# A hybrid attention layer on one core: weight preparations ordered behind earlier evacuations, with small edits at the start and the end

## The chip, the cores and the metric

The kernel runs on one core of one Trainium2 chip. The metric is the device time of one launch in microseconds, as the median of the runs that are shown. The engines are TensorE (PE in the rows, with its weight loads as PEld), VectorE (DVE), ScalarE (ACT), GpSimd (POOL) and SyncE (SP), which issues most of the DMA transfers. Each engine works through its own list of instructions in the order in which they stand in the program; across engines they wait for each other through semaphores.

## What is computed

One encoder layer runs on 512 tokens (256 of a prompt, 256 of a sample, each with 1024 channels). Everything is float32.

```python
h = _rmsnorm(x, attn_norm_gain)
proj = h @ w_in            # q,k,v; decay/beta; gates; latents; memory query; 3 merge gates
qkv = _centred_conv_silu(qkv, conv_w)
o_fwd = _gdn_chunked(q, k, v, g[:, :, 0], beta[:, :, 0])
o_bwd = _gdn_chunked(q[:, ::-1], k[:, ::-1], v[:, ::-1], g[:, ::-1, 1], beta[:, ::-1, 1])[:, ::-1]
o_gdn = _rmsnorm(o_fwd + o_bwd, gdn_norm_gain).reshape(b, s, W_GDN) * jax.nn.silu(z_gdn)
o_mla = _blocked_attention(q_full, k_full, v_mla, (D_NOPE + D_ROPE) ** -0.5).reshape(b, s, W_MLA) * jax.nn.silu(z_mla)
o_mem = jnp.einsum("bhqk,bkhd->bqhd", p, vm).reshape(b, s, W_MEM) * jax.nn.silu(z_mem)
merged = gates[:, :, 0] * (o_gdn @ w_br_gdn) + gates[:, :, 1] * (o_mla @ w_br_mla) + gates[:, :, 2] * (o_mem @ w_br_mem)
return x + merged @ w_out   # then a final RMSNorm
```

Branch A is a bidirectional gated delta rule in chunks of 64 tokens with 8 heads, branch B a latent attention (MLA) with 8 heads, branch C an attention of 4 heads into 256 memory tokens for each half.

## The kernel before

**Products in three passes.** To keep float32 accuracy on fp32r operands, every operand of a product is held as a rounded high part and a low part, which is the remainder. A product is high x high, then low of the data x high of the weight, then high of the data x low of the weight: for a contraction of 1024 and 128 output channels that is 3 x 8 matmuls of 128x512 into one PSUM bank. In names, `wh_`/`wl_` are the parts of a weight and `hh`/`hl` those of the normalised input.

**A weight's way.** `weight()` (line 224) brings a weight of up to 128x1024 with one SP DMA into one of two raw buffers (`wr_...`), has ACT round it (`wh_...`, line 241) and has DVE subtract to get the low part (`wl_...`, line 244). Both are issued with a raised priority. `gemm()` (line 264) then issues the matmuls (line 276). The finished bank is evacuated, depending on the kind of product: `split()` makes a high part on ACT (line 252) and a low part on DVE (line 254) for the values `v`, keys `kn` and queries `qn` of MLA; the convolution copies it into `cz_...` on ACT (line 767) and goes on with taps on DVE and ACT (lines 769 to 778); gates get a tanh on ACT (lines 1223 and 1251).

**Stages and what sets the order.** `front()` does the memory values first (`mem_v()`, lines 379 to 430: memory tokens times a weight, with ten matmuls on a zero tile ahead of them), then the norms, latents and the two attentions, with convolution inputs and gates put in between. Here the tile scheduler places the instructions of every engine by its own simulation and by priorities. `middle()` is the delta rule with the remaining projections; its TensorE order is written out by `weave`, from lists of work in which a generator yields when it may go on, while the other engines' orders still come from the scheduler. `back()` has the branch products and `output()`, which multiplies by `w_out`, adds the residual and does the final norm, the last quarter of the tokens in two halves of 256 channels (lines 1383 to 1401). `issue_after(i)` fixes that an instruction stands behind `i` in the program on the same engine; it adds no semaphore.

**Places that the steps below touch.** The rounding and low part in `weight()` (lines 241 and 244); the evacuations named above; `attend` (lines 356 to 367), which multiplies attention weights by values with 12 matmuls of 128x256, of which 4 read the low part `pl_a`; `gdn_out` (line 1182), where a yield of 12 sets how much other TensorE work lies ahead of the matmul `so` (line 1185) that waits for the sum `rr` (line 1181); in `mem_v()` the memsets (lines 383 and 387), the ten `zp` matmuls (line 390) and the load of the parameters `prm` (line 405), which the scaling of the memory tokens reads (lines 419 and 420).

Of the kernel before, what the change touches and what calls it, by code (L numbers as in the profile page):

```python
# [181 lines left out]
class Layer:  # L182
    def __init__(self, tc, A):
        self.tc, self.nc, self.A, self.hold = tc, tc.nc, A, None


# [37 lines left out]
    def weight(self, src, n, name, pool=None, into=None):  # L224

        nc = self.nc
        raw = self.p0.tile([P, 1024], F32, tag="wr", bufs=2, name="wr_" + name)
# [4 lines left out]

        def place(t, own):
            if into is not None:
                return into[t == "wl_"]
            kw = {} if pool else {"tag": own, "bufs": 2}
            return (pool or self.p0).tile([P, 1024], F32R, name=t + name, **kw)

        hi = place("wh_", "wh")
        with self.tc.high_priority(offset=60):  # L240
            self.wround = nc.scalar.activation(hi[:, :n], raw[:, :n], AF.Copy).ins  # L241
            lo = place("wl_", "wl")
            with nullcontext() if self.hold is None else self.tc.issue_after(self.hold):
                self.wsplit = nc.vector.tensor_tensor(lo[:, :n], raw[:, :n], hi[:, :n].bitcast(F32),  # L244
                                                      op=ALU.subtract).ins
            self.hold = None
        return hi, lo

    def split(self, src, hi, lo, scale=1.0):

        nc = self.nc
        a = nc.scalar.activation(hi, src, AF.Copy, scale=scale)
        if isinstance(scale, float) and scale == 1.0:
            self.lsplit = nc.vector.tensor_tensor(lo, src, hi.bitcast(F32), op=ALU.subtract).ins
# [65 lines left out]
    def attend(self, h, s, score, scale, vs, op, name):  # L320
# [40 lines left out]
        self.plast = self.lsplit  # L361
        n = 0
        for kb in range(2):
            q = slice(kb * 256, (kb + 1) * 256)
            for a, b in ((vs[kb][0], hi), (vs[kb][0], lo), (vs[kb][1], hi)):
                nc.tensor.matmul(pairs(op), a, turns(b[:, q]), start=n == 0, stop=n == 5)
                n += 1

# [10 lines left out]
    def mem_v(self):  # L379
        nc, A = self.nc, self.A  # L380
        ms = []
        warm = self.p0.tile([P, 1], F32, name="warm")
        nc.vector.memset(warm, 0.0)
        nc.scalar.activation(warm, warm, AF.Square)

        zero = self.s2("zero", F32R)
        nc.vector.memset(zero.bitcast(F32), 0.0)
        zp = self.ps_kk("zp")
        for i in range(10):
            nc.tensor.matmul(zp, zero[:, 0:P], zero, start=i == 0, stop=i == 9)  # L390

# [312 lines left out]
    def mla_v(self, g):  # L704
# [4 lines left out]
        for tb in range(4):  # L709
# [52 lines left out]
    def conv(self, ps, f, dst, name):  # L762
# [3 lines left out]
        with self.tc.high_priority(offset=60):  # L766
            nc.scalar.activation(z, ps.rearrange("p (s t) -> p s t", s=2), AF.Copy)
        y = dst
# [377 lines left out]
    def gdn_out(self, hh):  # L1146
# [32 lines left out]
        with self.behind():  # L1179
            nc.vector.transpose(out=st, in_=sq)  # L1180
            nc.vector.tensor_reduce(red, st.rearrange("p (j i) -> p j i", i=32), axis=AX.X, op=ALU.add)
        yield 0.0, 13 if hh == 7 else 12
        ssp = self.ps_ms(par, f"so{hh}")
# [36 lines left out]
    def silu2(self, dst, ps):  # L1220

        with self.tc.high_priority(offset=60):
            self.nc.scalar.activation(dst, ps, AF.Tanh, scale=0.5)
            self.nc.vector.scalar_tensor_tensor(dst, dst, 1.0, ps, ALU.add, ALU.mult)

# [19 lines left out]
    def gate(self, j, d):  # L1245
# [4 lines left out]
        with self.tc.high_priority(offset=60):  # L1250
            self.nc.scalar.activation(th, ps, AF.Tanh, scale=0.5)
        return th
# [69 lines left out]
    def output(self):  # L1322
# [399 lines left out]
```

## Time and profile before

| what | value |
|---|---|
| runs | 798.55, 798.67 and 798.84 us, median 798.67 us |
| profiled execution | 798.48 us, of which the span from first to last instruction is 796.7 us |
| granted TensorE clock, mean | 0.999 of full speed |
| PE busy | 786.6 us, 99% of the span, 4774 matmul records |
| PEld busy (beside PE) | 692.9 us, 87% |
| DVE busy | 579.2 us, 73% |
| ACT busy | 447.4 us, 56% |
| POOL busy | 166.9 us, 21% |
| DMA | 118.18 MB, mean 148 GB/s |

A row of the timeline gives start, duration, engine, line, operation, output and inputs, shapes and count (in us); behind it in brackets the idle time of that engine just before and what ended it. Matmuls overlap in the rows: one of 128x512 is shown with 0.38 us and the next starts 0.216 us after it. A row of the waits gives who waited for whom: total, times, longest.

### The profile page before, as it was taken

Reading aid. Unit: us, or ns where it says so; the run is one execution under the profiler, and the core shown is the slowest. Engines: PE = TensorE matmul, PEld = TensorE weight load, DVE = VectorE, ACT = ScalarE, POOL = GpSimd, SP = SyncE. Lnnn points to the kernel's source line nnn. Section 1 sums busy time; section 2 is a strip of 40 time slices with the busy share of each in tenths; the row PEclk is TensorE's granted clock in tenths of the full one; section 3 lists DMA queues with packets and bytes.
Section 4 is the critical chain, followed back from the end, with each engine's and each line's share of the span. In section 5 each row is a group of like instructions: output and inputs, shape, how many; then the busy total and the mean of one; then the engine's idle time right before and its main releaser. Section 6 shows DMA issues by size and latency. Waiting matters only on the chain.

```text
span 796.7 us, 13067 instructions
## 1 busy us (share of the span) xinstructions
PE 786.6 (99%) x4774; PEld 692.9 (87%) x4774; DVE 579.2 (73%) x974; ACT 447.4 (56%) x894; POOL 166.9 (21%) x135
## 2 busy tenths in 40 slices
PE   9999999999999999999999999999999999999996
PEld 7888898889898899988888888888888888888886
DVE  7886358787699999669599989498565655465543
ACT  6755465556565565646757556667766463322332
POOL 0200111000010002154221226540512003333312
PEclk9999999999999999999999999999999999999999
DMA  9523222732417635444444435555653557464532
GB/s 325 177 78 102 93 77 81 229 124 70 116 61 211 192 96 141 142 133 154 129 155 133 146 120 160 172 151 175 192 172 119 172 181 256 160 197 153 178 107 105
DMA packets 68911, 118.18 MB, mean 148 GB/s; under 512 B 23664, under 2 KB 31344, under 8 KB 68848
## 3 DMA queue, kind: packets, MB, share of 16 engines
q1 hardware_dynamic: 67552, 115.03, 45.9%
q10 hardware_dynamic: 1296, 2.33, 0.8%
q8 instruction: 37, 0.61, 0.3%
q14 instruction: 26, 0.21, 0.1%
HBM read 98.24 MB, written 19.09 MB: 147 GB/s over the span
## 4 chain that ended last, share of the span: by engine, by line
PE 91%; DVE 4%; DMA 1%; ACT 1%; issue 1%; POOL 0%; SPq 0%; POOLq 0%; ACTq 0%; DVEq 0%
PE gm_qkv L276 14%; PE gm_g L276 14%; PE gm_z L276 7%; PE gm_za L276 5%; PE gm_bm L276 5%; PE y L1345 5%; PE vm L427 3%; PE gm_be L276 3%; PE gm_qm L276 3%; PE gm_km L276 3%; PE gm_bg L276 3%; PE o L1163 2%; PE gm_bg L1312 2%; PE s_a L330 2%; PE kk L1012 2%; PE gm_qn L276 2%
## 5 line engine op out<-in xcount | busy, mean ns | idle before, releaser
L776 DVE SCALAR_TENSOR_TENSOR kq<-cz,prm,kq 128x510 f32<-128x510 f32 (+1 forms) x64 | 52.0, 813 | 2.2 <-ACT kq L769 1.3
L276 PE MATMUL gm_qkv<-hl,wh_qkv 128*128 128x512 f32 x192 | 49.0, 385 | 0.0
L276 PE MATMUL gm_g<-hh,wl_g 128*128 128x512 f32 x192 | 48.8, 384 | 0.0
L276 PE MATMUL gm_g<-hh,wh_g 128*128 128x512 f32 x192 | 48.0, 385 | 0.0
L276 PE MATMUL gm_g<-hl,wh_g 128*128 128x512 f32 x192 | 47.2, 382 | 0.0
L276 PE MATMUL gm_qkv<-hh,wl_qkv 128*128 128x512 f32 x192 | 47.0, 382 | 0.0
L276 PE MATMUL gm_qkv<-hh,wh_qkv 128*128 128x512 f32 x192 | 46.8, 381 | 0.0
L1287 POOL TENSOR_TENSOR mg<-mg,lg 128x512 f32<-128x512 f32 x16 | 29.5, 1849 | 73.2 <-DVE lg L1286 31.8
L244 DVE TENSOR_TENSOR wl_g<-wr_g,wh_g 128x1024 fp32r<-128x1024 f32 x24 | 31.2, 1300 | 17.1 <-PE gm_g L276 9.3
L244 DVE TENSOR_TENSOR wl_qkv<-wr_qkv,wh_qkv 128x1024 fp32r<-128x1024 f32 x24 | 31.0, 1290 | 13.6 <-ACT wh_qkv L241 7.7
L1022 DVE SCALAR_TENSOR_TENSOR ne<-e,cc,kk 128x512 f32<-128x512 f32 (+1 forms) x64 | 35.7, 608 | 6.2 <-ACT ed L843 2.7
L276 PEld LDWEIGHTS gm_qkv<-hh,wh_qkv 128*128 128x128 f32 x192 | 35.8, 189 | 5.1 <-ACT wh_qkv L241 0.3
L276 PEld LDWEIGHTS gm_g<-hl,wh_g 128*128 128x128 f32 x192 | 35.9, 189 | 4.7
L276 PEld LDWEIGHTS gm_qkv<-hh,wl_qkv 128*128 128x128 f32 x192 | 35.8, 189 | 4.8
L276 PEld LDWEIGHTS gm_g<-hh,wh_g 128*128 128x128 f32 x192 | 35.4, 189 | 4.8
L276 PEld LDWEIGHTS gm_qkv<-hl,wh_qkv 128*128 128x128 f32 x192 | 35.4, 189 | 4.7
L276 PEld LDWEIGHTS gm_g<-hh,wl_g 128*128 128x128 f32 x192 | 35.4, 189 | 4.5
L969 POOL TENSOR_SCALAR_AFFINE_SELECT e<-e 128x256 f32<-128x256 f32 x32 | 20.0, 651 | 90.2 <-DMA e<-d_r 75.1
L1345 PE MATMUL y<-wh_wo,mh 128*128 128x512 f32 (+1 forms) x144 | 37.7, 356 | 0.0
L241 ACT ACTIVATE wh_g<-wr_g 128x1024 fp32r<-128x1024 f32 x24 | 25.3, 1052 | 19.9 <-PE gm_g L276 7.2
L1188 POOL TENSOR_TENSOR rr<-rr,cst 32x16 f32<-32x16 f32 x8 | 25.0, 3123 | 46.6 <-DVE rr L1187 46.4
L241 ACT ACTIVATE wh_qkv<-wr_qkv 128x1024 fp32r<-128x1024 f32 x24 | 25.3, 1055 | 15.1 <-DVE vf L776 3.2
(458 smaller groups left out, 2189.4 us busy)
## 6 DMA issues: line engine op xcount, KB each, us to landing
wr_g<-in_w_dram SPq DMA_DIRECT2D x24, 512.0 KB, 4.0
wr_qkv<-in_w_dram SPq DMA_DIRECT2D x24, 512.0 KB, 3.8
e<-d_r SPq DMA_DIRECT2D x64, 96.0 KB, 3.0
wr_z<-in_w_dram SPq DMA_DIRECT2D x12, 512.0 KB, 3.6
d_g<-gt_g SPq DMA_DIRECT2D x16, 256.0 KB, 2.5
wr_za<-in_w_dram SPq DMA_DIRECT2D x8, 512.0 KB, 3.6
lg<-d_g SPq DMA_DIRECT2D x16, 256.0 KB, 3.9
wr_bm<-in_w_dram SPq DMA_DIRECT2D x8, 512.0 KB, 3.8
```

What stands on the lines that cost most here:

```text
L241: self.wround = nc.scalar.activation(hi[:, :n], raw[:, :n], AF.Copy).ins
L244: self.wsplit = nc.vector.tensor_tensor(lo[:, :n], raw[:, :n], hi[:, :n].bitcast(F32), op=ALU.subtract).ins
L276: nc.tensor.matmul(pairs(ps[:m]), a[:, k * m:(k + 1) * m], turns(xs[k][j]), start=n == 0, stop=n == 3 * nk - 1)
L330: nc.tensor.matmul(pairs(sp[:, qb * 256:(qb + 1) * 256]), a, turns(b), start=j == 0, stop=j == n - 1)
L427: nc.tensor.matmul(pairs(vps[tb]), ms[k][a][:, t], turns(b[:, :512]), start=k == 0 and i == 0, stop=k == 7 and i == 2)
L776: nc.vector.scalar_tensor_tensor(ys, zs, self.cw[:, f, m:m + 1], ys, ALU.mult, ALU.add)
L969: self.nc.gpsimd.affine_select(out=e[:, :, r], in_=e[:, :, r], pattern=[[0, 2], [sg, 128]], compare_op=ALU.is_ge, fill=NEG, base=0, channe ...
L1012: nc.tensor.matmul(pairs(ps), a[:, k], turns(b), start=i == 0, stop=i == 2)
L1022: nev = nc.vector.scalar_tensor_tensor(ne[:, :, d, s, r], es[d][:, s, r].unsqueeze(1).to_broadcast([P, 2, n]), cc[:, d, w:w + 1], kin, ALU ...
L1188: nc.gpsimd.tensor_tensor(rr, rr, c("hf")[last, 0:1].to_broadcast([32, 16]), op=ALU.pow)
L1287: nc.gpsimd.tensor_tensor(self.merged[d], self.merged[d], gt, op=ALU.add)
L1345: nc.tensor.matmul(pairs(ps), xs[2 * j + q][a][:, t], turns(b[:, q * 512:(q + 1) * 512])[:, c0 // 2:c1 // 2], start=j == 0 and n == 0, sto ...
```

## The change

**Order of the weight preparations.** Two lists (`self.bank`) hold the evacuations of the last products. `free()` registers the ACT and DVE instructions that empty a PSUM bank: both of `split()` for the MLA values, keys and queries, the copy into `cz_...`, the tanh of the gates and, in `silu2`, the DVE step behind it. At a call of `weight()` for product n, its rounding and low part are put behind those that were registered for product n-2, by `issue_after` for ACT and DVE. Then the lists move on by one.

**Smaller edits.** In `attend` the last attention of all (`a71`) takes its matmuls with the low part `pl_a` last. In `mem_v()` the zero tile is 128x128 in place of 128x512 and its memset comes first; the ten `zp` matmuls read it four times over by broadcast. The `prm` load is issued on POOL's queue in place of SP's second place. In `gdn_out` the yield of 12 becomes 13 for head 5 too. The last quarter of `output()`: a single matmul of 128x256 and a DVE copy put the residual into PSUM ahead of the products of the second half, so that ACT squares and sums straight from PSUM (in place of a DVE add and a DVE square with sum), a DVE step on 128x1 finishes the mean, and at the end DVE scales 256 channels from PSUM and 288 in SBUF while ACT scales 480 (before: 576 and 448).

```diff
 hi = place("wh_", "wh")
-        with self.tc.high_priority(offset=60):
+        with self.tc.high_priority(offset=60), ExitStack() as st:
+            for i in self.bank[0]:
+                st.enter_context(self.tc.issue_after(i))
+            self.bank = [self.bank[1], []]
             self.wround = nc.scalar.activation(hi[:, :n], raw[:, :n], AF.Copy).ins
...
+    def free(self, *a):
+        self.bank[1] += [i.ins for i in a]
...
-            self.split(ps, vh, vl)
+            self.free(*self.split(ps, vh, vl))
...
-            self.split(unpaired(ps), halves(hi), halves(lo))
+            self.free(*self.split(unpaired(ps), halves(hi), halves(lo)))
...
-            nc.scalar.activation(z, ps.rearrange("p (s t) -> p s t", s=2), AF.Copy)
+            self.free(nc.scalar.activation(z, ps.rearrange("p (s t) -> p s t", s=2), AF.Copy))
...
-            self.nc.scalar.activation(th, ps, AF.Tanh, scale=0.5)
+            self.free(self.nc.scalar.activation(th, ps, AF.Tanh, scale=0.5))
...
+        order = [(kb, i, b) for kb in range(2) for i, b in ((0, hi), (0, lo), (1, hi))]
+        if name == "a71":
+            order.sort(key=lambda o: o[2] is lo)
...
+        zero = self.s2("zero", F32R)[:, 0:P]
+        nc.vector.memset(zero.bitcast(F32), 0.0)
         warm = self.p0.tile([P, 1], F32, name="warm")
...
-            nc.tensor.matmul(zp, zero[:, 0:P], zero, start=i == 0, stop=i == 9)
+            nc.tensor.matmul(zp, zero, zero.unsqueeze(1).to_broadcast([P, 4, P]), start=i == 0, stop=i == 9)
...
-                    nc.sync.dma_start(self.prm, A["prm"])
+                    nc.gpsimd.dma_start(self.prm, A["prm"])
...
-        yield 0.0, 13 if hh == 7 else 12
+        yield 0.0, 13 if hh in (5, 7) else 12
...
+        product(parts[1], *ws[0], 0, 3, 256, 512, 1)
+        nc.vector.tensor_copy(parts[1], y)
...
-        nc.vector.tensor_tensor(y, y, ps[:, 0:256], op=ALU.add)
-        nc.vector.tensor_tensor_reduce(self.ct("jk")[:, 0:256], y, y, 1.0 / D, s3[:, 0:1], ALU.mult, ALU.add, s3[:, 2:3])
+        nc.scalar.activation(self.ct("jk")[:, 0:256], ps, AF.Square, accum_out=s3[:, 2:3])
+        nc.vector.tensor_scalar(s3[:, 2:3], s3[:, 2:3], 1.0 / D, s3[:, 0:1], ALU.mult, ALU.add)
...
-        nc.vector.tensor_scalar(ys[3][:, 448:1024], ys[3][:, 448:1024], r, None, ALU.mult)
+        nc.vector.scalar_tensor_tensor(y, ps, r, fg[:, 768:1024], ALU.mult, ALU.mult)
+        nc.vector.tensor_scalar(ys[3][:, 480:768], ys[3][:, 480:768], r, None, ALU.mult)
```

**How instructions move, first place: ACT in `front()`**, around the MLA products that the trace has at 158 to 168 us. A name is a tile with its number; `cz_1733<-gm_qkv_1707` empties the bank of the product that uses `wh_qkv_1703`, and `wh_qkv_1764` is the weight two products later. Before:

```order
L241 ACTIVATE wh_qkv_1703<-wr_qkv_1701 128x1024
L252 ACTIVATE vh_1681<-v_1674 128x512
L241 ACTIVATE wh_qn_1744<-wr_qn_1742 128x384
L252 ACTIVATE kn_1698<-gm_kn_1691 128x512
L241 ACTIVATE wh_qkv_1764<-wr_qkv_1762 128x1024
L777 ACTIVATE cz_1654<-kq_1653 128x512
L767 ACTIVATE cz_1733<-gm_qkv_1707 128x512
```

and after the change:

```order
L256 ACTIVATE vh_1681<-v_1674 128x512
L245 ACTIVATE wh_qkv_1703<-wr_qkv_1701 128x1024
L256 ACTIVATE kn_1698<-gm_kn_1691 128x512
L245 ACTIVATE wh_qn_1744<-wr_qn_1742 128x384
L783 ACTIVATE cz_1654<-kq_1653 128x512
L773 ACTIVATE cz_1733<-gm_qkv_1707 128x512
L245 ACTIVATE wh_qkv_1764<-wr_qkv_1762 128x1024
```

Before, the rounding `wh_qkv_1764` stands two rows ahead of the evacuation `cz_1733`; now it stands right behind it. The same goes for `wh_qkv_1703`, which is now behind `vh_1681`.

**Second place: TensorE beside it**, from the end of the product `gm_qkv_1707` to the start of `gm_qkv_1768`. Before:

```order
L276 MATMUL gm_qkv_1707<-hh_386,wl_qkv_1705 128x512
L276 MATMUL gm_qn_1748<-qlh_823,wh_qn_1744 128x512
L276 MATMUL gm_qn_1748<-qlh_859,wh_qn_1744 128x512
L276 MATMUL gm_qn_1748<-qlh_897,wh_qn_1744 128x512
L276 MATMUL gm_qn_1748<-qll_824,wh_qn_1744 128x512
L276 MATMUL gm_qn_1748<-qll_860,wh_qn_1744 128x512
L276 MATMUL gm_qn_1748<-qll_898,wh_qn_1744 128x512
L276 MATMUL gm_qn_1748<-qlh_823,wl_qn_1746 128x512
L276 MATMUL gm_qn_1748<-qlh_859,wl_qn_1746 128x512
L276 MATMUL gm_qn_1748<-qlh_897,wl_qn_1746 128x512
L276 MATMUL gm_qkv_1768<-hh_339,wh_qkv_1764 128x512
```

and after the change:

```order
L284 MATMUL gm_qkv_1707<-hh_379,wl_qkv_1705 128x512
L284 MATMUL gm_qkv_1707<-hh_386,wl_qkv_1705 128x512
L284 MATMUL gm_qn_1748<-qlh_823,wl_qn_1746 128x512
L284 MATMUL gm_qn_1748<-qlh_859,wl_qn_1746 128x512
L284 MATMUL gm_qn_1748<-qlh_897,wl_qn_1746 128x512
L284 MATMUL gm_qkv_1768<-hh_339,wh_qkv_1764 128x512
```

Before, nine matmuls of the query product `gm_qn_1748` lie between the last matmul of `gm_qkv_1707` and the first of `gm_qkv_1768`; now three do, since the scheduler has put the first six ahead of the low pass of `gm_qkv_1707`.

**Third place: ACT in the middle**, which the trace has at 590 to 598 us; `gt_g_6508<-gm_g_6436` is the tanh of a merge gate and `wh_g_6582` the weight two products later. Before:

```order
L1142 ACTIVATE ub_5962<-us_6420 64x2x128 x2
L252 ACTIVATE xg_6461<-og_6046 128x512
L241 ACTIVATE wh_g_6582<-wr_g_6580 128x1024
L1068 ACTIVATE p1s_6495<-p_6478 128x128
L1079 ACTIVATE y_3752<-y_5470 32x4x32 x8
L1054 ACTIVATE m_3753<-ne_6323 64x2x64 x2
L1174 ACTIVATE kq_3734<-kq_3734 128x2x256
L992 ACTIVATE kh_6559<-kq_4110 128x512
L992 ACTIVATE kh_6563<-kq_4110 128x512
L1251 ACTIVATE gt_g_6508<-gm_g_6436 128x512
L1172 ACTIVATE sq_6532<-o_6520 128x512
L241 ACTIVATE wh_be_6636<-wr_be_6634 128x512
```

and after the change:

```order
L1148 ACTIVATE ub_5962<-us_6420 64x2x128 x2
L256 ACTIVATE xg_6461<-og_6046 128x512
L1074 ACTIVATE p1s_6495<-p_6478 128x128
L1085 ACTIVATE y_3752<-y_5470 32x4x32 x8
L1060 ACTIVATE m_3753<-ne_6323 64x2x64 x2
L1180 ACTIVATE kq_3734<-kq_3734 128x2x256
L998 ACTIVATE kh_6559<-kq_4110 128x512
L998 ACTIVATE kh_6563<-kq_4110 128x512
L1257 ACTIVATE gt_g_6508<-gm_g_6436 128x512
L245 ACTIVATE wh_g_6582<-wr_g_6580 128x1024
L1178 ACTIVATE sq_6532<-o_6520 128x512
L245 ACTIVATE wh_be_6636<-wr_be_6634 128x512
```

The rounding `wh_g_6582` has moved from ahead of `p1s_6495` to behind the tanh `gt_g_6508`, seven rows on. TensorE's order is the same there.

More of the change, by code (lines that the diff above doesn't have):

```diff
@@ L253, in split @@
         if isinstance(scale, float) and scale == 1.0:
-            self.lsplit = nc.vector.tensor_tensor(lo, src, hi.bitcast(F32), op=ALU.subtract).ins
-        else:
-            nc.vector.scalar_tensor_tensor(lo, src, scale, hi.bitcast(F32), ALU.mult, ALU.subtract)
-        return a
+            b = nc.vector.tensor_tensor(lo, src, hi.bitcast(F32), op=ALU.subtract)
+            self.lsplit = b.ins
+        else:
+            b = nc.vector.scalar_tensor_tensor(lo, src, scale, hi.bitcast(F32), ALU.mult, ALU.subtract)
+        return a, b
+    def free(self, *a):
+        self.bank[1] += [i.ins for i in a]
     def gemm_fm(self, src, nk, xs, name, m=P, ps=None):
@@ L361, in attend @@
         self.plast = self.lsplit
[L362 to L367, printed above, removed]
+        order = [(kb, i, b) for kb in range(2) for i, b in ((0, hi), (0, lo), (1, hi))]
+        if name == "a71":
+            order.sort(key=lambda o: o[2] is lo)
+        for n, (kb, i, b) in enumerate(order):
+            nc.tensor.matmul(pairs(op), vs[kb][i], turns(b[:, kb * 256:(kb + 1) * 256]), start=n == 0, stop=n == 5)
     def setup(self):
@@ L384, in mem_v @@
         nc.scalar.activation(warm, warm, AF.Square)
-        zero = self.s2("zero", F32R)
-        nc.vector.memset(zero.bitcast(F32), 0.0)
-        zp = self.ps_kk("zp")
+        zp = self.ps_kk("zp").rearrange("p (a b) -> p a b", a=4)
         for i in range(10):
-            nc.tensor.matmul(zp, zero[:, 0:P], zero, start=i == 0, stop=i == 9)
+            nc.tensor.matmul(zp, zero, zero.unsqueeze(1).to_broadcast([P, 4, P]), start=i == 0, stop=i == 9)
         vps = [self.ps_gm(f"vm{tb}") if tb == 3 else self.ps_ms(tb % 2, f"vm{tb}") for tb in range(4)]
@@ L1222, in silu2 @@
         with self.tc.high_priority(offset=60):
-            self.nc.scalar.activation(dst, ps, AF.Tanh, scale=0.5)
-            self.nc.vector.scalar_tensor_tensor(dst, dst, 1.0, ps, ALU.add, ALU.mult)
+            self.free(self.nc.scalar.activation(dst, ps, AF.Tanh, scale=0.5),
+                      self.nc.vector.scalar_tensor_tensor(dst, dst, 1.0, ps, ALU.add, ALU.mult))
     def mla_gate(self, h):
@@ L1338, in output, with product @@
             ss.append(self.pe.tile([P, 4], F32, name=f"yss{tb}"))
-        def product(ps, hi, lo, j, tb, c0=0, c1=512):
+        def product(ps, hi, lo, j, tb, c0=0, c1=512, last=24, seeded=False):
             t = slice(tb * P, (tb + 1) * P)
@@ L1344, in product @@
                 for a, b in ((0, hi), (1, hi), (0, lo)):
-                    nc.tensor.matmul(pairs(ps), xs[2 * j + q][a][:, t],
-                                     turns(b[:, q * 512:(q + 1) * 512])[:, c0 // 2:c1 // 2],
-                                     start=j == 0 and n == 0, stop=j == 3 and n == 5)
+                    if 6 * j + n < last:
+                        nc.tensor.matmul(pairs(ps), xs[2 * j + q][a][:, t],
+                                         turns(b[:, q * 512:(q + 1) * 512])[:, c0 // 2:c1 // 2],
+                                         start=j == 0 and n == 0 and not seeded, stop=j == 3 and n == 5)
                     n += 1
@@ L1381, in output @@
             nc.sync.dma_start(out[:, 512:1024], y)
-        s3, out = ss[3], A["ys"][0, P:2 * P]
-        for q in range(2):
-            ps = self.ps_kk(f"y2{q}")
+        s3, out, y = ss[3], A["ys"][0, P:2 * P], ys[3][:, 768:1024]
+        parts = [self.ps_kk(f"y2{q}")[:, 0:256] for q in range(2)]
+        product(parts[1], *ws[0], 0, 3, 256, 512, 1)
+        nc.vector.tensor_copy(parts[1], y)
+        for q, ps in enumerate(parts):
             for j in range(4):
-                product(ps[:, 0:256], *ws[j], j, 3, 256 * q, 256 * q + 256)
+                product(ps, *ws[j], j, 3, 256 * q, 256 * q + 256, 24, q == 1)
             if q == 0:
-                y = add(ps[:, 0:256], 3, 2, 256)
+                x = add(ps, 3, 2, 256)
                 nc.vector.tensor_scalar(s3[:, 0:1], s3[:, 1:2], 1.0 / D, s3[:, 0:1], ALU.mult, ALU.add)
-                nc.gpsimd.tensor_tensor(y, y, fg[:, 512:768], op=ALU.mult)
-        y = ys[3][:, 768:1024]
-        nc.vector.tensor_tensor(y, y, ps[:, 0:256], op=ALU.add)
-        nc.vector.tensor_tensor_reduce(self.ct("jk")[:, 0:256], y, y, 1.0 / D, s3[:, 0:1], ALU.mult, ALU.add, s3[:, 2:3])
+                nc.gpsimd.tensor_tensor(x, x, fg[:, 512:768], op=ALU.mult)
+        nc.scalar.activation(self.ct("jk")[:, 0:256], ps, AF.Square, accum_out=s3[:, 2:3])
+        nc.vector.tensor_scalar(s3[:, 2:3], s3[:, 2:3], 1.0 / D, s3[:, 0:1], ALU.mult, ALU.add)
         r = self.pe.tile([P, 1], F32, tag="fr", bufs=4, name="fr3")
         nc.gpsimd.tensor_tensor(r, s3[:, 2:3], self.c("hf")[:, 0:1], op=ALU.pow)
-        nc.vector.tensor_tensor(y, y, fg[:, 768:1024], op=ALU.mult)
-        nc.scalar.activation(ys[3][:, 0:448], ys[3][:, 0:448], AF.Copy, scale=r)
-        nc.scalar.dma_start(out[:, 0:448], ys[3][:, 0:448])
-        nc.vector.tensor_scalar(ys[3][:, 448:1024], ys[3][:, 448:1024], r, None, ALU.mult)
-        nc.sync.dma_start(out[:, 448:1024], ys[3][:, 448:1024])
+        nc.scalar.activation(ys[3][:, 0:480], ys[3][:, 0:480], AF.Copy, scale=r)
+        nc.scalar.dma_start(out[:, 0:480], ys[3][:, 0:480])
+        nc.vector.scalar_tensor_tensor(y, ps, r, fg[:, 768:1024], ALU.mult, ALU.mult)
+        nc.vector.tensor_scalar(ys[3][:, 480:768], ys[3][:, 480:768], r, None, ALU.mult)
+        nc.sync.dma_start(out[:, 480:1024], ys[3][:, 480:1024])
     def run(self):
```

1 line of the change is left out of this document (added).

## Prediction

> **What bounds the kernel now.** I read the page first (busy time, then the chain that ended last), then the waits of PE, then the timeline at the places that these name and at those where the change moves a rounding.
>
> ```profile
> PE 786.6 (99%) x4774; PEld 692.9 (87%) x4774; DVE 579.2 (73%) x974; ACT 447.4 (56%) x894; POOL 166.9 (21%) x135
> PE 91%; DVE 4%; DMA 1%; ACT 1%; issue 1%; POOL 0%; SPq 0%; POOLq 0%; ACTq 0%; DVEq 0%
> ```
>
> TensorE is busy for 99% of the span and carries 91% of the chain. ACT and DVE set the time only where TensorE stands still for them, so the question is which such stops go and which come. The waits of PE name all stops that there are:
>
> ```profile
> PE zp L390 <- DVE zero L387: 1.5, 1, 1.5
> PE gm_qn L276 <- DVE kn L254: 0.9, 1, 0.9
> PE kk L1012 <- DVE ne L1022: 0.5, 1, 0.5
> PE s_m L330 <- ACT p_m L344: 0.5, 1, 0.5
> PE oa L366 <- DVE pl_a L254: 0.3, 1, 0.3
> PE so L1185 <- DVE rr L1181: 0.3, 1, 0.3
> ```
>
> They add up to 4.0 us, 1.5 of them before the first matmul. Not one row has TensorE waiting for a weight's rounding (line 241) or low part (line 244). So the part of the change that orders the preparations can remove at most the one wait for `kn`, while it works on something that costs nothing today because it is early.
>
> **What a later rounding costs.** The unit comes from the first place shown in the order, 156 to 160 us:
>
> ```profile
> 156.72 1.03 PE L276 MATMUL gm_qkv<-hh,wl_qkv 128*128 128x512 f32 x4
> 158.45 0.59 PE L717 MATMUL v<-wl_wv,klh 128*128 128x512 f32 x2
> 160.22 1.99 PE L276 MATMUL gm_qkv<-hh,wh_qkv 128*128 128x512 f32 x8
> 157.85 0.60 ACT L767 ACTIVATE cz<-gm_qkv 128x512 f32<-128x512 f32 x1 [1.37 <-PE gm_qkv L276]
> 158.48 0.73 ACT L769 ACTIVATE kq<-cz,prm 128x512 f32<-128x512 f32 x1
> 159.12 1.05 ACT L241 ACTIVATE wh_qkv<-wr_qkv 128x1024 fp32r<-128x1024 f32 x1
> ```
>
> The last of the four `gm_qkv` matmuls starts at 156.72 + 3 x 0.216 = 157.37; ACT's evacuation starts 0.48 later, at 157.85, and holds ACT for 0.5 to 0.63. A rounding takes 1.05 (159.12 to 160.17), and TensorE uses it 0.05 later, at 160.22. If the rounding stands right behind the evacuation of a product whose last matmul starts at T, the weight can be used at T + 0.48 + 0.5 + 1.05 + 0.05 = T + 2.08. With m matmuls of 128x512 in between, TensorE asks at T + 0.216 (m + 1). Only from m = 9 on is the rounding free. Counting m in the new order gives these waits in `front()`:
>
> 1. 160.22: the rounding is now behind `vh`, whose `v` product has its last matmul at 158.67. `vh` starts at 159.15, the rounding at 159.65, and the weight can be used at 160.75 in place of 160.22: 0.5 us, or 0.7 since the convolution's last matmul also comes one later. I take 0.6.
> 2. The next weight of that kind (before: used at 167.44) is behind `cz_1733`, with m = 3: 2.08 - 0.86 = 1.2 us, or 1.35 with the longer hold. I take 1.25.
> 3. A gate's weight, used at 264.59, is behind four steps of ACT: the evacuation, the convolution's two next steps, and `vh`.
>
> ```profile
> 259.61 0.60 ACT L767 ACTIVATE cz<-gm_qkv 128x512 f32<-128x512 f32 x1 [1.31 <-PE gm_qkv L276]
> 260.87 0.62 ACT L777 ACTIVATE cz<-kq 128x512 f32<-128x512 f32 x1
> 263.06 1.06 ACT L241 ACTIVATE wh_g<-wr_g 128x1024 fp32r<-128x1024 f32 x1 [1.58 <-PE v L717]
> 264.59 1.89 PE L276 MATMUL gm_g<-hh,wh_g 128*128 128x512 f32 x8
> ```
>
> T is 259.13. After 260.87 follow 0.5 for that step and 0.5 for `vh`, so the rounding starts at 261.9 and the weight is ready at 263.0, T + 3.87. In the new order 12 matmuls stand between, T + 2.81: 1.05 us. The step at 260.87 needs DVE's taps, so up to 2.0; I take 1.1.
> 4. The weight used at 272.86 is behind the tanh `gt_g`, m = 3: 1.2 us.
> 5. The weight used at 288.69 is behind the tanh `za`, m = 3 and four small transposes, some 0.35 us more of cover: 0.85 us.
>
> In the middle TensorE's order is nearly unchanged and the waits are read from the rows alone:
>
> ```profile
> 356.39 0.64 ACT L777 ACTIVATE cz<-kq 128x512 f32<-128x512 f32 x1 [7.75 <-DVE kq L776]
> 356.93 1.05 ACT L241 ACTIVATE wh_g<-wr_g 128x1024 fp32r<-128x1024 f32 x1
> 358.15 1.89 PE L276 MATMUL gm_g<-hh,wh_g 128*128 128x512 f32 x8
> 552.93 0.45 PE L1064 MATMUL p<-t,ne 32*32 32x32 f32 x32
> 556.21 0.27 ACT L1068 ACTIVATE p1s<-p 128x128 f32<-128x128 f32 x1
> 561.12 0.58 ACT L1223 ACTIVATE zt_z<-gm_z 128x512 f32<-128x512 f32 x1
> 560.13 0.59 PE L276 MATMUL gm_g<-hh,wh_g 128*128 128x512 f32 x2
> 591.18 0.45 PE L1064 MATMUL p<-t,ne 32*32 32x32 f32 x32
> 591.71 0.28 ACT L1068 ACTIVATE p1s<-p 128x128 f32<-128x128 f32 x1
> 596.63 0.58 ACT L1251 ACTIVATE gt_g<-gm_g 128x512 f32<-128x512 f32 x1
> 597.11 0.59 ACT L1172 ACTIVATE sq<-o 128x512 f32<-128x512 f32 x1
> 597.54 1.46 PE L276 MATMUL gm_g<-hh,wh_g 128*128 128x512 f32 x6
> 646.22 0.38 ACT L1122 ACTIVATE u<-u 128x256 f32<-128x256 f32 x1 [1.34 <-PE u L1120]
> 648.42 2.18 ACT L252 ACTIVATE xa<-xa 128x512 fp32r<-128x512 f32 x4
> 648.83 1.46 PE L276 MATMUL gm_g<-hh,wh_g 128*128 128x512 f32 x6
> ```
>
> 6. 358.15: the tanh goes ahead of the rounding, 0.48 (596.63 to 597.11 is a tanh's hold): 356.93 + 0.48 + 1.05 + 0.05 = 358.51, a wait of 0.35.
> 7. 560.13: the rounding goes behind the tanh `zt_z`. `p1s` now stands ahead of two steps that it waited behind, so it can start when `p` ends, 553.4. From `p1s` to `zt_z` ACT had 4.9 us of work; with the two steps (about 1.1) the tanh starts at 559.4, the weight is ready at 561.0: 0.9, between 0.5 and 1.2.
> 8. 597.54: here ACT runs without a gap from `p1s`, which cannot start before `p` ends (591.63). The rounding takes the place of `sq` at 597.11, is ready at 598.21: 0.67.
> 9. 648.83: likewise from `u`; the rounding starts at 648.42: 0.69.
>
> The nine add up to 7.6 us. Who waits is TensorE, with all that is queued behind the matmul. The low parts on DVE move back as well; they are asked for 16 matmuls (3.5 us) after the high parts, so I take nothing, and up to 1.5 for the high end, with places that just miss my list (219.67, m = 9).
>
> **What the change removes.**
>
> ```profile
> 268.37 0.52 ACT L241 ACTIVATE wh_qn<-wr_qn 128x384 fp32r<-128x384 f32 x1 [3.76 <-DMA wr_qn<-in_w_dram]
> 269.27 0.59 ACT L252 ACTIVATE kn<-gm_kn 128x512 fp32r<-128x512 f32 x1
> 272.21 0.81 PE L276 MATMUL gm_qn<-qlh,wl_qn 128*128 128x512 f32 x3
> 128.10 0.35 DVE L622 TENSOR_TENSOR ga<-gl,cst 128x64 fp32r<-128x64 f32 x2
> ```
>
> `kn` was queued behind a rounding that waited 3.76 us for its DMA; now it stands ahead of it, and the wait of 0.9 goes. `so` gets five more matmuls ahead, 1.08 us against 0.3 to 0.5: -0.4. `oa` gets three matmuls of 0.11 ahead: -0.33. The wait of `s_m` does not go with it: those matmuls moved back, and now the small product `rp` follows at once, which needs DVE's `ga`, ready at 128.1 to 128.5 as before. I take +0.2, between -0.5 and +1.3. `kk` stays: 0, at best -0.5.
>
> The start and the end:
>
> ```profile
> 1.49 4.63 PE L390 MATMUL zp<-zero 128*128 128x512 f32 x10 [1.49 <-DVE zero L387]
> 5.53 0.91 ACT L419 ACTIVATE mh<-memT,prm 128x256 fp32r<-128x256 f32 x2 [2.84 <-DMA prm<-in_prm_dram]
> 6.09 0.87 PE L427 MATMUL vm<-wh_vm,mh 128*128 128x512 f32 x2
> ```
>
> The smaller memset lets `zp` start about 0.5 earlier, but `zp` only fills the time until `vm`, which waits for `mh` and so for `prm`. No transfer in the trace is issued by POOL. Its landing lies between that of a load issued first of all (a gain of 0.4, bounded by the end of `zp`) and 0.4 later than now; I take -0.3, as `prm` leaves its second place in the queue. The Trainium skill, "DMA: Bandwidth & Descriptors" (the table at its head), gives the GpSimd path about 1 us to the first byte against about 0.6 for the other; by that, an estimate, the gain would shrink to nothing and the sum rise by 0.3. At the end ACT's square saves a step, the two scalings behind the power cost one more, and one matmul of 0.11 is added: +0.1, within 0.4 either way.
>
> Together: -0.9 - 0.4 - 0.33 + 0.2 - 0.3 + 0.1 = -1.6 us. The sum is 7.6 - 1.6 = +6.0. The profiled execution took 798.48 us (span 796.7, and 1.8 around it), 0.2 below the median of 798.67; on the median the forecast is 804.7 us.
>
> **Rivals.**
>
> *Not slower: the roundings still come in time.* If TensorE found at least nine matmuls between each evacuation and the next weight, only the removals would count: 798.67 - 1.6 = 797.0 us. For it speaks that no wait of PE names a rounding today. Against it stands the new order with m = 3 in three places. Chance 0.04.
>
> *Partial: the waits eat each other.* A stop of TensorE gives DVE and ACT time to catch up, so places bound by DVE (3, 6, parts of 7) could vanish, and the first stop of a pair could cover the second. The five that hang on TensorE's own last matmul or on `p` and `u` (2, 4, 5, 8, 9) move with TensorE and cannot. They make 4.7 us, or 3.1 net if the others go: 801.5. If they too were halved, +1 remained, within what can be told from no change. Chance 0.10, half of it for the latter.
>
> *More: DVE becomes the bound from 120 to 290 us.* The new order puts conv steps, which need DVE, ahead of roundings on ACT. If DVE is late by 1 to 2 us at two or three of these places, 3 to 5 us come on top: 808 to 810. Chance 0.13.
>
> *The clock.* After the 0.9 us wait at `gm_qn` the three matmuls at 272.21 are still 0.216 apart (0.65 to 272.86), so a wait of this size leaves the clock alone. The Trainium skill, "TensorE: Matmul & The Clock Gate" (section on psum-queue depth-cycling), tells of a kernel whose short idle times between groups of matmuls brought the clock down again and again. If each of eight waits cost some 1.7 us that way, it would be 818. Chance 0.01.
>
> That the ordering is not in force can be excluded: the rows show it.
>
> **The numbers.** The forecast has 0.72. The range goes from the partial case (801.3) to the case with DVE (809.5); left out are the 0.04, the lower half of the partial case, the clock and a part of the case with DVE. Runs of this kernel differ by 0.3 us, and 0.2% or 1.6 us is what can be told from no change. Faster by more: 0.04; within: 0.05; slower: 0.91.
>
> **What would show it.** The waits of PE in the changed kernel should list `gm_qkv` and `gm_g` behind ACT `wh_qkv` and `wh_g` (line 245) with about 1.2 us at the longest and some 7 us in all, and no `gm_qn` behind `kn`. The forecast is wrong if these rows are absent or add up to less than 3 us, or if low parts (line 248) lead the list.

## The result and the profile after

The changed kernel takes 810.65 us (median of 5 runs, 808.31 to 813.89), the kernel before 798.67 us in the same session (5 runs, 798.43 to 799.14). The ratio is 1.015, with a 95% interval of 1.0132 to 1.0168: 12.0 us slower, twice the forecast of 6.0, and above the range's end of 809.5. The profiled execution of the changed kernel took 811.23 us with a span of 809.4, 12.7 longer than the span before.

From the page of the changed kernel, the engines' busy times and the chain that ended last:

```profile
PE 789.0 (97%) x4775; PEld 692.0 (85%) x4775; DVE 577.2 (71%) x973; ACT 441.1 (54%) x896; POOL 170.1 (21%) x136
PE 66%; DVE 17%; ACT 5%; DMA 5%; issue 3%; POOL 2%; SPq 0%; POOLq 0%; ACTq 0%; DVEq 0%
```

TensorE's work is the same to 2.4 us, but it now fills 97% of the span instead of 99%, and the chain that ended last runs through it for 66% instead of 91%. The other engines are in the chain because TensorE waits for them. Its waits in the changed kernel (total, times, longest):

```profile
PE gm_qkv L284 <- ACT wh_qkv L245: 3.8, 4, 1.0
PE gm_g L284 <- ACT wh_g L245: 3.5, 4, 1.4
PE so L1191 <- DVE rr L1187: 1.6, 1, 1.6
PE vm L433 <- ACT mh L425: 1.5, 1, 1.5
PE gm_qn L284 <- ACT wh_qn L245: 1.4, 2, 0.7
PE zp L396 <- DVE warm L392: 1.1, 1, 1.1
PE gm_kn L284 <- DVE wl_kn L248: 0.8, 1, 0.8
PE rp L633 <- DVE ga L628: 0.8, 1, 0.8
```

The first two rows are the forecast ones: 7.3 us for roundings of `qkv` and `g` weights, where before there was none. The rows of `so`, `vm`, `gm_qn` and `gm_kn`, 5.3 us in all, stand nowhere in the forecast, unless under "up to 1.5" for the high end.

**A forecast wait, at the place with three matmuls in between.** TensorE and ACT in the changed kernel:

```profile
169.51 1.89 PE L284 MATMUL gm_qkv<-hh,wl_qkv 128*128 128x512 f32 x8
171.24 0.81 PE L284 MATMUL gm_qn<-qlh,wl_qn 128*128 128x512 f32 x3
173.03 1.13 PE L284 MATMUL gm_qkv<-hh,wh_qkv 128*128 128x512 f32 x4 [0.98 <-ACT wh_qkv L245]
...
171.44 0.60 ACT L773 ACTIVATE cz<-gm_qkv 128x512 f32<-128x512 f32 x1 [1.41 <-PE gm_qkv L284]
171.93 1.05 ACT L245 ACTIVATE wh_qkv<-wr_qkv 128x1024 fp32r<-128x1024 f32 x1
```

The last matmul of `gm_qkv` starts at 169.51 + 7 x 0.216 = 171.02 (T). The evacuation starts at T + 0.42, the rounding at T + 0.91, and the weight is used at T + 2.01, where the prediction's unit was T + 2.08. ACT itself was idle for 1.41 us ahead of `cz`, and the load of this weight had landed at 169.62: the rounding could have been done there, and the ordering forbids it.

**An unforeseen wait through a load.** SP, DVE, ACT and TensorE of the changed kernel at 160 to 168 us, and SP in the kernel before:

```profile
161.79 0.80 SPq L704 DMA_DIRECT2D qs<-d_q  x2
162.68 0.84 SPq L707 DMA_DIRECT2D qs<-d_q  x2
163.63 0.36 SPq L230 DMA_DIRECT2D wr_qn<-in_w_dram  x1
...
161.63 0.42 DVE L248 TENSOR_TENSOR wl_kn<-wr_kn,wh_kn 128x256 fp32r<-128x256 f32 x1
...
167.54 0.52 ACT L245 ACTIVATE wh_qn<-wr_qn 128x384 fp32r<-128x384 f32 x1 [3.40 <-DMA wr_qn<-in_w_dram]
...
162.10 0.70 PE L284 MATMUL gm_kn<-klh,wl_kn 128*128 128x512 f32 x2 [0.78 <-DVE wl_kn L248]
168.11 0.92 PE L284 MATMUL gm_qn<-qlh,wh_qn 128*128 128x512 f32 x3 [0.69 <-ACT wh_qn L245]
```

```profile
159.00 0.37 SPq L229 DMA_DIRECT2D wr_qn<-in_w_dram  x1
```

The low part `wl_kn` is late on DVE and ends at 162.05; TensorE waits 0.78 for it. The load of the `qn` weight is issued at 163.63 instead of at 159.00. ACT then stands 3.40 us at `wh_qn`, and TensorE 0.69.

What holds this load up is SP's queue, and the delay begins some 20 us earlier. The same engines there, after and then before:

```profile
140.29 0.53 ACT L245 ACTIVATE wh_rb<-wr_rb 128x384 fp32r<-128x384 f32 x1
141.28 0.55 DVE L248 TENSOR_TENSOR wl_rb<-wr_rb,wh_rb 128x384 fp32r<-128x384 f32 x1
141.86 0.33 SPq L230 DMA_DIRECT2D wr_wv<-in_wv_dram  x1
...
156.22 0.38 SPq L701 DMA_DIRECT2D d_q<-rh  x1
```

```profile
132.50 0.52 ACT L241 ACTIVATE wh_rb<-wr_rb 128x384 fp32r<-128x384 f32 x1
...
135.50 0.33 SPq L229 DMA_DIRECT2D wr_wv<-in_wv_dram  x1
```

The rounding `wh_rb` is now behind the tanh of a gate (started at 139.81), 7.79 us later than before, some 1.4 of it from the late start and the wait of `rp`. Its low part `wl_rb` is the last reader of the raw buffer that `wr_wv` is to fill, and the load is issued 0.03 us after `wl_rb` ends, in both kernels: 141.86 instead of 135.50. From there the lateness is handed on: the low part of that weight ends at 149.80 (before: 143.91), the step `rh`, which waits for DVE steps queued behind it, starts at 151.16 (144.54), and SP writes the next `rh` out to `d_q` in memory at 156.22 (149.96). The four loads of `qs` read `d_q` back and wait until that write has landed (161.77), and the load of `wr_qn` stands directly behind them, as it did before the change. The end of `wl_kn` at 162.05 did not hold it. A second wait for a `qn` weight, at 276.22 (0.68), looks alike at its end: the load is issued at 273.13, behind `qs` loads that wait for such a write to land (272.19). It was not followed further back.

**An unforeseen wait on DVE's way.** Before, at the merge of the block at 522 to 529 us, and after, at 530 to 539:

```profile
523.07 1.42 DVE L244 TENSOR_TENSOR wl_z<-wr_z,wh_z 128x1024 fp32r<-128x1024 f32 x1
527.42 0.69 DVE L1181 TENSOR_REDUCE rr<-st 128x16 f32<-128x512 f32 x1
528.85 0.29 PE L1185 MATMUL so<-rr,cst 128*128 128x16 f32 x2
```

```profile
531.07 0.58 ACT L773 ACTIVATE cz<-gm_qkv 128x512 f32<-128x512 f32 x1
531.55 1.05 ACT L245 ACTIVATE wh_z<-wr_z 128x1024 fp32r<-128x1024 f32 x1
...
532.63 1.22 DVE L248 TENSOR_TENSOR wl_z<-wr_z,wh_z 128x1024 fp32r<-128x1024 f32 x1 [0.74 <-ACT wh_z L245]
538.17 0.68 DVE L1187 TENSOR_REDUCE rr<-st 128x16 f32<-128x512 f32 x1
539.00 0.36 PE L1191 MATMUL so<-rr,cst 128*128 128x16 f32 x2 [1.60 <-DVE rr L1187]
```

The rounding `wh_z` is now behind `cz`. DVE, which takes its instructions in order, stands 0.74 us for it at `wl_z`, and the sum `rr` that TensorE needs is queued behind that. The victim is not the weight's own product but a small matmul that has nothing to do with the weight.

**The start.** POOL, ACT and TensorE of the changed kernel; before, `mh` started at 5.53 and `vm` at 6.09:

```profile
1.25 0.75 POOL L411 DMA_DIRECT2D prm<-in_prm_dram  x1 [0.80 <-POOLq L1719]
6.66 0.91 ACT L425 ACTIVATE mh<-memT,prm 128x256 fp32r<-128x256 f32 x2 [3.98 <-DMA prm<-in_prm_dram]
7.22 2.32 PE L433 MATMUL vm<-wh_vm,mh 128*128 128x512 f32 x8 [1.53 <-ACT mh L425]
```

`mh` waits for the parameters and starts 1.13 us later than when SP loaded them in its second place. Two things come together here: POOL's issue ends at 2.00 instead of 1.60, and SP now issues a second `memT` load in the old place of `prm`, which lands at 6.21, ahead of `prm`. No run separates them.

### The profile page after: what moved, and what is told of

It reads as the page before. It is cut to its first block, busy times and chain, and to the rows that moved or that the text cites. A ratio compares the mean times of both kernels' runs of the same rounds, so it can differ in the third digit from the quotient of the medians.

```text
span 809.4 us, 13054 instructions
## 1 busy us (share of the span) xinstructions
PE 789.0 (97%) x4775; PEld 692.0 (85%) x4775; DVE 577.2 (71%) x973; ACT 441.1 (54%) x896; POOL 170.1 (21%) x136
## 4 chain that ended last, share of the span: by engine, by line
PE 66%; DVE 17%; ACT 5%; DMA 5%; issue 3%; POOL 2%; SPq 0%; POOLq 0%; ACTq 0%; DVEq 0%
PE gm_g L284 13%; PE gm_qkv L284 8%; PE gm_bm L284 5%; PE y L1352 4%; PE gm_za L284 3%; PE gm_qm L284 3%; PE gm_km L284 3%; PE gm_bg L284 3%; PE vm L433 3%; PE gm_bg L1318 2%; PE gm_be L284 2%; PE gm_z L284 2%; PE gm_cq L284 2%; DVE ne L1028 2%; DVE kq L782 2%
## 5 line engine op out<-in xcount | busy, mean ns | idle before, releaser
L248 DVE TENSOR_TENSOR wl_qkv<-wr_qkv,wh_qkv 128x1024 fp32r<-128x1024 f32 x24 | 33.3, 1387 | 9.6 <-ACT wh_qkv L245 9.4
L1257 ACT ACTIVATE gt_g<-gm_g 128x512 f32<-128x512 f32 x24 | 14.2, 592 | 40.3 <-PE gm_g L284 30.8
L284 PE MATMUL gm_bm<-xa,wh_bm 128*128 128x512 f32 x112 | 28.9, 382 | 0.0
```

Source lines behind the costliest of these rows:

```text
L284: nc.tensor.matmul(pairs(ps[:m]), a[:, k * m:(k + 1) * m], turns(xs[k][j]), start=n == 0, stop=n == 3 * nk - 1)
L1257: self.free(self.nc.scalar.activation(th, ps, AF.Tanh, scale=0.5))
```

## The experiments

Theory A: the ordering makes the 12 us, by late roundings and by what hangs on late preparations (loads, DVE's queue); the smaller edits make next to nothing. Theory B, the rival: the ordering makes the forecast 6 to 8 us, and the smaller edits (POOL's load, the last quarter) the rest. Later runs split theory A. Each ratio is to the kernel before on the same chip, which took 798.5 to 799.0 us there. All kernels compute the whole reference.

**1. The change without the ordering.**

```
-            for i in self.bank[0]:
-                st.enter_context(self.tc.issue_after(i))
```

> The changed kernel without the ordering of roundings and low parts; all smaller edits stay. Theory A (the ordering makes nearly all of the +12.0 us; the smaller edits only the late start, 7.22 in place of 6.09): 799.0 to 799.8 us, with no wait of PE for a rounding. Theory B (the smaller edits, or the altered first microseconds that shift everything behind them, make half or more of it): 804 us or more.

799.78 us, ratio 1.0009 (0.9996 to 1.0022). TensorE's waits in it, without the one ahead of the first matmul:

```profile
PE vm L431 <- ACT mh L423: 1.4, 1, 1.4
...
PE kk L1016 <- DVE ne L1026: 0.7, 1, 0.7
PE s_m L336 <- ACT p_m L350: 0.5, 1, 0.5
```

Every wait for a rounding, the two of `gm_qn`, that of `gm_kn` and that of `so` are gone. Theory B falls: without the ordering the change cannot be told from the kernel before.

**2. The kernel before with the ordering alone.** The `bank` lists, the loop and the calls of `free` from the diff, nothing else of it.

> The kernel before with the ordering of roundings and low parts alone. Theory A: 809.5 to 811 us, with the waits for wh_qkv, wh_g and wh_qn, for wl_kn and for the sum rr at the places where the changed kernel has them, and vm starting at 6.1. Theory B: 804 us or less.

810.42 us, ratio 1.0139 (1.0118 to 1.016). Its four largest waits:

```profile
PE gm_g L284 <- ACT wh_g L245: 3.5, 4, 1.4
PE gm_qkv L284 <- ACT wh_qkv L245: 3.4, 4, 1.0
PE so L1193 <- DVE rr L1189: 2.2, 2, 1.9
PE gm_qn L284 <- ACT wh_qn L245: 2.0, 2, 1.2
```

The ordering alone costs what the whole change costs. The waits are not the same to the tenth: here `gm_kn` has none and `gm_qn` has 0.6 more, most of it at its second place (1.15 at 274.54 instead of 0.68 at 276.22).

**3. The change with the parameter load back on SP.**

```
-                    nc.gpsimd.dma_start(self.prm, A["prm"])
+                    nc.sync.dma_start(self.prm, A["prm"])
```

> The changed kernel with the parameter load back on SP's queue in second place. If the load on POOL's queue makes the late start: vm starts at 6.1 or earlier and the time falls by 1.1 to 1.5 us, to about 809.3. If the start is late for another reason (the smaller memset, the other loads): vm stays at 7.2 and the time at 810.6.

808.82 us, ratio 1.0116 (1.0092 to 1.0141); its profiled execution 810.37, against 811.23 with POOL's load. `vm` starts at 5.93, 1.29 us earlier than with POOL's load, but the last matmul only 0.73 (802.52 against 803.25), because the wait of `gm_kn` is 1.13 here instead of 0.78 and the first of `gm_qn` 1.10 instead of 0.69: TensorE came earlier to places where others set the time. POOL's load costs 0.7 to 0.9 us by the profiles and 1.8 by the medians; the intervals of the two ratios overlap.

**4. The ordering three weights back instead of two.**

```
-            self.bank = [self.bank[1], []]
+            self.bank = [self.bank[1], self.bank[2], []]
...
-        self.bank[1] += [i.ins for i in a]
+        self.bank[2] += [i.ins for i in a]
```

> The changed kernel with the ordering against the evacuations of three weights back in place of two. Theory A in the form that too few matmuls lie between an evacuation and the next weight: with one product more between them the waits for roundings go, and 799.5 to 801.5 us are left, the late start among it. Theory C (any such ordering holds up ACT and DVE, whose queues then make the low parts, the loads and rr late): 804 to 808 us, with waits for wl_kn, wh_qn behind its load, and rr still there.

801.95 us, ratio 1.0029 (1.0014 to 1.0043). With one weight more of distance, the waits for `qkv`, `kn` and `qn` and that of `so` are gone. Left on weights are two waits of `gm_g` for `wh_g`, 1.0 us together; besides there are 0.5 us at `ra`. That the distance is what decides, as the unit T + 2.08 says, is borne out. The kernel is still 3.1 us slower than the one before, with POOL's load in it, and 0.45 above the range that was expected.

**5. The smaller edits alone, with the parameter load on SP.** Runs 1 and 3 together.

> The changed kernel without the ordering and with the parameter load back on SP's queue: the smaller memset, the last attention, head 5's sum and the last quarter are left. If the late start of the run without the ordering was the load's alone: vm at 5.9 to 6.1, no matmul at the slow rate behind it, and 797.3 to 798.3 us, 0.5 to 1.5 below the kernel before. If the smaller edits bring nothing: 798.8.

798.36 us, ratio 0.9996 (0.9987 to 1.0004): not to be told from the kernel before, and on the edge of the gain that was expected. Its idle time of TensorE behind the first matmul is 2.2 us, against 2.6.

**6. The ordering in the middle of the program only** (parameter load on SP, as in all runs from here on).

```
-            for i in self.bank[0]:
+            for i in self.bank[0] if self.banks == 4 else []:
```

> As the changed kernel with the parameter load on SP, the ordering in force only in the middle stage. If each wait belongs to its own place: the four waits of 539, 571, 610 and 661 us stay (4.0 us idle, about 4.7 with the slower restart), the five to seven of the front go, and the time is 802.5 to 803.5 us. If the waits of the middle are an after-effect of the front's (its late loads and low parts): they go too, and 798 to 800 us are left.

801.69 us, ratio 1.0036 (1.001 to 1.0061). Its waits on the ordering:

```profile
PE gm_g L284 <- ACT wh_g L245: 2.4, 3, 1.4
PE so L1191 <- DVE rr L1187: 1.8, 1, 1.8
```

The three gates' weights (1.36, 0.50, 0.58) and `so` wait here as in the whole change, although nothing is late in front of them. They belong to their own places and are no after-effect of `front()`. The time is 0.8 below the range that was expected for that.

**7. Only DVE's part of the ordering:** the weights are ordered behind the DVE evacuations alone, so ACT's hold nothing back. Behind `cz_...` and the merge gates' tanh, which register ACT alone, nothing is ordered any more.

```
-        self.bank[1] += [i.ins for i in a]
+        self.bank[1] += [i.ins for i in a[1:]]
```

> As the changed kernel with the parameter load on SP, the ordering for DVE's low parts alone (ACT's roundings free). If the rounding behind the evacuation is what costs: no wait for wh_qkv or wh_g, and 798 to 800 us. If the low parts and the raw buffers that they free late cost as much: waits for wl and for wh_qn behind its load, 802 us or more.

801.01 us, ratio 1.0024 (1.0012 to 1.0036), about 2.6 us above run 5. TensorE, ACT and SP at the largest of the waits on weights:

```profile
168.42 1.78 PE L284 MATMUL gm_qkv<-hh,wh_qkv 128*128 128x512 f32 x7 [1.03 <-ACT wh_qkv L245]
167.31 1.06 ACT L245 ACTIVATE wh_qkv<-wr_qkv 128x1024 fp32r<-128x1024 f32 x1 [1.83 <-DMA wr_qkv<-in_w_dram]
162.36 0.35 SPq L230 DMA_DIRECT2D wr_qkv<-in_w_dram  x1
```

For comparison, the same rounding in run 5, which TensorE uses at 167.59 without a wait:

```profile
165.57 1.06 ACT L243 ACTIVATE wh_qkv<-wr_qkv 128x1024 fp32r<-128x1024 f32 x1 [2.64 <-DMA wr_qkv<-in_w_dram]
```

A wait named as one for ACT's rounding is one for a load here: ACT had been free for 1.83 us. The load was issued at the end of the low part `wl_qkv`, at 162.36 against 162.09 in run 5, and landed 4.85 us later against 3.38. So the rounding is 1.74 later, and the issue behind the low part accounts for only 0.27 of that; why the transfer took longer is not shown. I had expected no wait for `wh_qkv` at all, and 798 to 800 us, or else 802 and more; the time lies between. Another 1.5 us are at `gm_z` (at 473.98), for an evacuation that ACT has queued behind eight other steps; its cause was not followed further. The DVE part of the ordering thus costs by itself, while the prediction priced it at nothing, but by which path is not shown. What ACT's part would cost alone stays open, and so does a third raw buffer, which would take the loads off the low parts: neither was run.

**8. The ordering for the `qn` weights only,** to keep the one gain that the ordering was forecast to bring.

```
-            for i in self.bank[0]:
+            for i in self.bank[0] if name[:2] == "qn" else []:
```

> As the changed kernel with the parameter load on SP, the ordering only for the weights of the query products (qn), the place where the kernel before waited 0.9 us for kn. If the ordering helps where the rounding waits for its load and the evacuation does not: no wait of gm_qn for kn, none for a rounding, and 796.8 to 797.8 us. If ordering costs as such: 799 us or more.

798.84 us, ratio 0.9998 (0.9988 to 1.0008). The wait of `gm_qn` for `kn` is gone, and another stands 4 us ahead of its place:

```profile
265.26 1.06 ACT L245 ACTIVATE wh_g<-wr_g 128x1024 fp32r<-128x1024 f32 x1 [1.04 <-DMA wr_g<-in_w_dram]
266.37 1.99 PE L284 MATMUL gm_g<-hh,wh_g 128*128 128x512 f32 x8 [0.95 <-ACT wh_g L245]
```

No gain: 0.91 went and 0.95 came, by a load. The time lies between the two that were expected (up to 797.8, or 799 and more).

**9. Run 6 without the z weights,** to test the reading of `so`.

```
-            for i in self.bank[0] if self.banks == 4 else []:
+            for i in self.bank[0] if self.banks == 4 and name[0] != "z" else []:
```

> The ordering in the middle of the program only, as in the run before with the ordering in the middle (801.69 us), but the roundings and low parts of the z weights are left out of it, so that the rounding of the z block stands ahead of the evacuation cz again. Theory: the 1.78 us wait of so near 529 us comes from the late rounding and low part of the z weights on the way to DVE's chain that ends in rr; it falls to 0.3 us or less, while the waits for wh_g of 1.36, 0.50 and 0.58 us stay: 799.6 to 800.5 us. Rival: the wait of so is set by the other DVE work of that block and the late z weights are only beside it: so keeps 1.6 us or more, 801.4 to 802.

801.72 us, ratio 1.0059 (1.003 to 1.0088). DVE at the place in question, and two of TensorE's waits:

```profile
522.66 1.42 DVE L248 TENSOR_TENSOR wl_z<-wr_z,wh_z 128x1024 fp32r<-128x1024 f32 x1
527.01 0.69 DVE L1187 TENSOR_REDUCE rr<-st 128x16 f32<-128x512 f32 x1
```

```profile
PE kk L1018 <- DVE ne L1028: 1.2, 2, 0.8
PE so L1191 <- DVE rr L1187: 0.9, 1, 0.9
```

At 529 us the reading holds: DVE no longer stands for `wh_z`, `rr` starts 1.3 us earlier than in run 6 (528.34 there), and the wait of `so` there is gone. The time did not fall, though. The scheduler placed other steps of DVE anew, and a wait of `kk` at 473 to 475 (1.2) and another of `so` at 494.7 (0.9) took the place of the 1.8; at the latter, `rr` now stands behind two steps (491.62 to 493.99) that it stood ahead of in run 6. The mechanism was right at 529, the forecast of 799.6 to 800.5 wrong.

**10. Run 5 with 13 matmuls on the first memset instead of 10.**

```
-        for i in range(10):
+        for i in range(13):
```

> The smaller edits with the parameter load on SP and no ordering, with 13 instead of 10 matmuls on the first memset, so that TensorE is busy until the first vm matmul can start. Theory: the idle time ahead of vm (1.07 us in the run with 10) goes, the vm matmuls behind it show no spacing of 350 ns or more, and the time is 0.3 to 1 us below that run's 798.36: 797.4 to 798.1 us. Rival: the start is set by the landing of the parameter load and not by the state of TensorE: the first real work begins at the same time and the time is the same, 798.2 to 798.5.

798.06 us, ratio 0.9998 (0.9984 to 1.0013). `vm` starts at 6.09 after an idle time of 0.22, in run 5 at 6.21 after 1.07. The idle time is mostly filled, but `vm` starts only 0.12 earlier: the landing of the parameters sets the start (5.56 in run 5, 5.44 here, with `mh` 0.09 behind it in both). The median lies in the range that was expected for a gain over run 5 (797.4 to 798.1), but against the kernel before on its own chip it is 0.4 lower here and 0.6 lower in run 5, so no gain is shown. The wait for `kn`, absent in run 5, is back with 0.77 at 270.73: it hangs on when the load of `wr_qn` lands, and comes and goes between kernels that do not touch it.

None of these versions beats the kernel before by more than its interval.

## Why the prediction was right in direction and wrong in size

**The nine waits: eight came, and near their size.** Eight of the nine places are in the trace. Forecast against the idle time shown, in the order of the list: 0.6 and 0.91; 1.25 and 0.98; 1.1 and 1.05; 1.2 and 1.04; 0.85 and 0.86; 0.9 and 1.36; 0.67 and 0.50; 0.69 and 0.58. Together 7.26 and 7.28. Place 6 (0.35) did not come: the step ahead of the tanh started 2.19 us before TensorE asked (364.75 to 366.94) instead of 1.76 (356.39 to 358.15), so the later rounding was just in time. This is the "waits eat each other" of the partial rival, at one place of the three that it named. A wait costs some 0.16 more than the idle time shown: ahead of 173.03 two matmuls start 173.03 - 171.67 = 1.36 us apart instead of 0.216, while the row shows 0.98. The forecast counted from when TensorE asks to when the weight can be used, which includes this 0.16. So its 7.26 is to be held against 7.28 + 8 x 0.16 = 8.6: the closeness of the two sums is luck, and two single places (0.6 and 0.9 forecast) are short by some 0.5 to 0.6.

**The low parts and the loads, taken as nothing: wrong.** This is the step that failed. The sentence "they are asked for 16 matmuls (3.5 us) after the high parts, so I take nothing" looks only at the product that uses the low part, and even there it holds only for weights with a contraction of 1024: `gm_kn` has two matmuls to a pass, so its low part is asked for 4 matmuls (0.86 us) after the high part. Beyond its product, a low part is the last reader of a raw buffer, so that the next load waits for it (`wl_rb` and `wr_wv`), and it stands in DVE's queue ahead of steps of other chains. A rounding that is put back makes its low part, and so the load, late as well. In the prediction's sum, what a preparation holds up besides its own product stood at nothing. It is what shows at `gm_kn` (0.78), `gm_qn` twice (1.37; the first followed back to `wl_rb`, the second not) and `so` (1.60): 3.75 us, over twice the 1.5 that was held back for it. Run 9 shows that `so` hung on the late preparation of z. Run 7 shows that ordering on DVE alone costs time, but not that it does so through the loads. How the 3.75 divide between late rounding and late low part at each place is not settled: the waits moved from place to place in every variant.

**The start, -0.3: wrong.** `vm` starts 1.13 us later, outside the bounds of -0.4 to +0.4. Their lower end was a load that SP issues first of all and their upper end a guess without a row. POOL's issue takes 0.75 where SP's takes 0.42, and the load lands later still, now behind a second `memT` load of SP. The page of the Trainium skill that the prediction quoted ("DMA: Bandwidth & Descriptors", table at the head) had the sign right with 1 against 0.6 us to the first byte; the traces show 1.13 to 1.29 from end to end for this load, the changed order of the loads included.

**What goes: right, and a little more.** The waits of `kn` (0.91), `oa` (0.35) and `so` at 635 (0.31) went as forecast; `kk` (0.52), forecast to stay, went too in this kernel. `s_m` was replaced by `rp`, 0.76 for 0.50 (forecast +0.2). But runs 1, 5 and 10 show how little this is worth: `kk`, `s_m` and `kn` come and go from kernel to kernel, and all the smaller edits together cannot be told from nothing.

**The sum.** From the idle times: 7.28 + 3.75 + 1.13 + 0.26 - 2.09 = 10.3; eight more stops than before at 0.16 each make 1.3. That is 11.6 of the 12.7 by which the spans differ. Against the forecast's +6.0 the largest differences are the low parts and loads (+3.75), the start (+1.4) and the waits on roundings (8.6 for 7.6). The remaining 1.1 lie in spacings of single matmuls too short for the trace to list as waits, and no run puts them to a cause.

**The rivals.** "Not slower" fell with the first row of the waits, and the clock with it: behind the waits for `qkv`, `qn` and `kn` the first matmul takes 0.32 to the next and the following ones 0.216. "DVE becomes the bound" gave 808 to 810, near the 810.65, but for another reason: it put the extra time on the convolution's steps between 120 and 290 us. What came there was late loads and one low part, and the largest single extra was at 539. The time of the partial rival is misadded in the prediction: its net 3.1 us give 801.8, not 801.5 or 801.3. Nothing here hangs on it.

## What to carry to other kernels

A preparation that works ahead has slack toward its own consumer and holds several other things up: the buffer that it reads, the load behind that buffer, and the queue of its engine. When it is moved back, price each of these, by the row of the load's issue, what stands ahead of it on its queue, and the row of the next instruction on that queue that another engine waits for. And where a scheduler places instructions, the waits of under 1 us that a small edit removes come back elsewhere (runs 8 and 9); count such a gain only when the time shows it.

## What was not expected of the hardware

In run 1 the first matmuls on data still ran at half speed:

```profile
7.06 3.66 PE L431 MATMUL vm<-wh_vm,mh 128*128 128x512 f32 x8 [1.37 <-ACT mh L423]
```

From start to start the first step is 0.587, then come six of 0.426 to 0.427, then one of 0.350. In the changed kernel the stop at this place was longer (1.53), and the same eight steps took 2.15 in place of 3.50: 1.3 us lost in run 1. In both kernels the ten `zp` matmuls ahead of the stop are 0.427 apart from the second on, so the clock had not yet risen there. The trace's record of the granted clock has full speed from 10.47 us on in run 1, from 6.03 on in the changed kernel and from 6.46 on in the kernel before. So the length of the stop alone does not decide it. The Trainium skill, "TensorE: Matmul & The Clock Gate" (Part 1: The HAM clock gate), gives 426.7 ns at N = 512 for the half clock and has the rise set by a window of about 3.4 us that runs freely, so that the moment depends on where in the window the first matmul falls. The six steps agree with the spacing to the nanosecond; that the window's phase makes the difference is in keeping with the records, and no run here tests it.
